# The first y load of a multiply-and-GELU kernel, issued from the ACT queue beside the first x load

## Chip, cores and metric

One core of a Trainium2 chip. The metric is device time in microseconds (us) of one execution. Runs of one kernel differ by 0.3% for the kernel before (120.61 to 121.00 us); every run used here was fast, with a granted clock of 1.0. The experiments ran on three chips, each beside the kernel before. A difference is called faster or slower from 2% on; smaller ones are given with their 95% interval. A ratio is the mean time of one kernel's fast runs over the mean of the other's in the same rounds, so it is not quite the ratio of the medians that are quoted beside it.

## The reference

```python
batch, dim = 1024, 4096            # x, y: float32
z = x * y
return 0.5 * z * (1 + np.tanh(np.sqrt(2 / np.pi) * (z + 0.044715 * z ** 3)))
```

Two inputs of 16.8 MB are read and one output of 16.8 MB is written: 50.3 MB for eight multiplies and eight activations.

## The kernel before

Each tensor is viewed as 128 partitions of 32768 numbers. x and the result live in one buffer of that size; y comes through a ring buffer of half the size. I call the two x loads x0 and x1 (8.4 MB each) and the three y loads y0 (8.4 MB), y1 and y2 (4.2 MB each). `_hoist` moves a DMA issue ahead of the start-up barriers, the points at which the engines wait for one another before the kernel's own work (in the profile before, the two hoisted issues start at 0.00 and 0.43 us and the next one, x1's, at 1.92).

The profile's names: SP is SyncE, ACT is ScalarE, DVE is VectorE, POOL is GpSimd; SPq and ACTq are their instruction queues. What SyncE issues stands in these profiles under DMA queue q1, what ScalarE issues under q10 (41.94 and 8.39 MB in the changed kernel), and the page counts 16 DMA engines for both. A packet is one record of moved bytes. I call what one DMA engine moves of one queue a ring. Each transfer has 16 records of four bytes (112 for the 7 transfers before), by their count one from each DMA engine; I call them its completion signals, and it has landed when all 16 have come. `...` marks what is left out.

```python
X_LOADS = [(0, 16384), (16384, 32768)]
Y_LOADS = [(0, 16384, 0), (16384, 24576, 0), (24576, 32768, 8192)]
STEP = 4096
STORES = [(0, 16384), (16384, 32768)]
...
    _hoist(nc, [load_x(0).ins, load_y(0).ins])       # both on SyncE's queue
    load_x(1)
    for i in (1, 2):      # y1 after 2 multiplies, y2 after 4
        nc.sync.wait_ge(sem_mul, (Y_LOADS[i][1] - Y_LOADS[1][0]) // STEP)
        load_y(i)
...
    # for each y load: wait for the x and the y load, then per 4096 columns:
    #   VectorE multiplies, ScalarE applies the GELU
...
    for i, (a, b) in enumerate(STORES):              # after 4 and after 8 activations
        nc.sync.wait_ge(sem_act, b // STEP)
        nc.sync.dma_start(out=out_r[:, a:b], in_=xs[:, a:b]).then_inc(sem_o[i], 16)
```

Of the kernel before, what the change touches and what calls it, by code (L numbers as in the profile page):

```python
# [1 line left out]

# [4 lines left out]


F32 = mybir.dt.float32
GELU = mybir.ActivationFunctionType.Gelu_apprx_tanh  # L10
# [7 lines that stand above are left out]
Y_RING = 16384  # L18


def _hoist(nc, issued):

    here = nc.cur_bb.bb.instructions
    first = nc.main_func.blocks[0].instructions
    for ins in issued:
        del here[next(k for k, i in enumerate(here) if i is ins or i.name == ins.name)]
    engine = issued[0].engine
    at = next(
        k
        for k, i in enumerate(first)  # L30
        if i.engine == engine and type(i).__name__ == "InstDrain"
    )
    first[at:at] = issued


@with_exitstack
def kernel(
    ctx: ExitStack,
    tc: tile.TileContext,
    x: bass.AP,  # L40
    y: bass.AP,
    out: bass.AP,
):
    nc = tc.nc
    P = nc.NUM_PARTITIONS

    x_r = x.flatten_outer_dims().rearrange("(p a) c -> p (a c)", p=P)
    y_r = y.flatten_outer_dims().rearrange("(p a) c -> p (a c)", p=P)
    out_r = out.flatten_outer_dims().rearrange("(p a) c -> p (a c)", p=P)
    total_f = x_r.shape[1]  # L50


    tc.close()
    tc.compile()  # L54

    xs = nc.alloc_sbuf_tensor("xs", [P, total_f], F32).ap()
    ys = nc.alloc_sbuf_tensor("ys", [P, Y_RING], F32).ap()
    sem_x = [nc.alloc_semaphore(f"sem_x{i}") for i in range(len(X_LOADS))]
    sem_y = [nc.alloc_semaphore(f"sem_y{i}") for i in range(len(Y_LOADS))]
    sem_mul = nc.alloc_semaphore("sem_mul")  # L60
    sem_act = nc.alloc_semaphore("sem_act")
    sem_o = [nc.alloc_semaphore(f"sem_o{i}") for i in range(len(STORES))]

    def load_x(i):
        a, b = X_LOADS[i]
        return nc.sync.dma_start(out=xs[:, a:b], in_=x_r[:, a:b]).then_inc(sem_x[i], 16)  # L66

    def load_y(i):
        a, b, r = Y_LOADS[i]
        return nc.sync.dma_start(  # L70
            out=ys[:, r : r + b - a], in_=y_r[:, a:b]
        ).then_inc(sem_y[i], 16)

    _hoist(nc, [load_x(0).ins, load_y(0).ins])
    load_x(1)
    for i in (1, 2):
        nc.sync.wait_ge(sem_mul, (Y_LOADS[i][1] - Y_LOADS[1][0]) // STEP)
        load_y(i)

    n = 0  # L80
    for i, (a, b, r) in enumerate(Y_LOADS):
        for j, (xa, xb) in enumerate(X_LOADS):
            if xa <= a < xb:
                nc.vector.wait_ge(sem_x[j], 16)
        nc.vector.wait_ge(sem_y[i], 16)  # L85
        for c in range(a, b, STEP):
            nc.vector.tensor_mul(  # L87
                out=xs[:, c : c + STEP],
                in0=xs[:, c : c + STEP],
                in1=ys[:, r + c - a : r + c - a + STEP],  # L90
            ).then_inc(sem_mul, 1)
            n += 1
            nc.scalar.wait_ge(sem_mul, n)
            nc.scalar.activation(  # L94
                out=xs[:, c : c + STEP], in_=xs[:, c : c + STEP], func=GELU
            ).then_inc(sem_act, 1)

    for i, (a, b) in enumerate(STORES):
        nc.sync.wait_ge(sem_act, b // STEP)
        nc.sync.dma_start(out=out_r[:, a:b], in_=xs[:, a:b]).then_inc(sem_o[i], 16)  # L100
    for i in range(len(STORES) - 1):
        nc.sync.wait_ge(sem_o[i], 16)
    nums = sorted(s.num for s in [*sem_x, *sem_y, *sem_o[:-1], sem_mul, sem_act])
    assert nums == list(range(nums[0], nums[-1] + 1))
    nc.sync.sem_clear(range(nums[0], nums[-1] + 1))
    nc.sync.wait_ge(sem_o[-1], 16).then_inc(sem_o[-1], -16)


# [1 line left out]
_INS = ['x', 'y']  # L110
_OUTS = [((1024, 4096), 'float32')]


# [23 lines left out]
```

## Time and profile before

| | before |
|---|---|
| time, median of the first 3 runs | 120.87 us (120.85 to 120.92) |
| span in the profile | 119.3 us |
| VectorE / ScalarE busy | 29% / 25% |
| share of the 16 DMA engines' time with a packet | 98.7% |
| first multiply starts | 41.31 us |
| x1 landed; y1, y2 landed | 60.5; 70.3, 80.6 us |
| the two stores landed | 100.0, 119.3 us |

A landing is the issue's start plus the time to landing in that tensor's view. The rows that matter for the bound are the DMA digits (mean busy share of the 16 engines in forty slices, in tenths) and the queue row. The lines are in the prediction. One line each of the views of the x input and of the y buffer before:

```profile
DMA to landing us min/median/max: 21.9/40.3/58.6
```

```profile
DMA to landing us min/median/max: 20.2/21.9/40.8
```

In the first line the smallest is x0, the largest x1; in the second they are y1, y2 and y0, in this order. x0 is complete at 21.9 us, and nothing uses it until y0 is there too.

### The profile page before, as it was taken

The page shows a single profiled execution, that of the slowest core. Times are in us where ns is not written, and L with a number is a line of the kernel's source. Part 1 is how long each engine was busy: PE and PEld are TensorE (multiplying, and loading weights), DVE is VectorE, ACT ScalarE, POOL GpSimd, SP SyncE. Part 2 cuts the span into 40 slices and gives each one's busy share as a digit, 9 for nine tenths or more (in the row PEclk, how much of TensorE's full clock was granted, in tenths as well). Part 3 has the DMA queues.
Part 4 walks back from the last instruction along what each step waited for, and adds up shares of the span by engine and source line. Part 5 has one row for each costly group of instructions (what it writes and reads, how often), then busy time and mean ns, then how long its engine had stood idle before and what let it go on. Part 6 is the DMA issues. An engine that isn't in the chain of part 4 may idle for free.

```text
span 119.3 us, 68 instructions
## 1 busy us (share of the span) xinstructions
DVE 35.0 (29%) x8; ACT 30.2 (25%) x9; POOL 0.2 (0%) x4
## 2 busy tenths in 40 slices
DVE  0000000000000199999600049959990000000000
ACT  3000000000000006797790000977479200000000
POOL 0000000000000000000000000000000000000000
DMA  9899888998899889988898989998889888998894
GB/s 352 352 439 615 352 352 352 659 396 352 352 615 439 352 352 483 571 352 352 385 494 352 505 374 494 385 527 352 352 352 703 352 352 352 637 418 352 352 527 176
DMA packets 1008, 50.33 MB, mean 422 GB/s; under 512 B 112, under 2 KB 112, under 8 KB 112
## 3 DMA queue, kind: packets, MB, share of 16 engines
q1 hardware_dynamic: 1008, 50.33, 98.7%
HBM read 33.55 MB, written 16.78 MB: 422 GB/s over the span
## 4 chain that ended last, share of the span: by engine, by line
DMA 53%; DVE 22%; ACT 3%; SPq 0%; issue 0%; DVEq 0%
DMA ys<-in_y_dram 53%; DVE xs L87 22%; ACT xs L94 3%; SPq L66 0%; DVEq L85 0%
## 5 line engine op out<-in xcount | busy, mean ns | idle before, releaser
L87 DVE TENSOR_TENSOR xs<-xs,ys 128x4096 f32<-128x4096 f32 x8 | 35.0, 4420 | 54.5 <-DMA ys<-in_y_dram 54.5
L94 ACT ACTIVATE xs<-xs 128x4096 f32<-128x4096 f32 x8 | 28.9, 3617 | 61.0 <-DVE xs L87 61.0
L94 ACT ACT_TABLE_LOAD x1 | 1.3, 1283 | 1.9 <-PEq L54 1.9
L121 POOL MEMSET const-uint8-127<- 128x1 uint8 x1 | 0.1, 102 | 0.0
L121 POOL MEMSET const-bfloat16-1.0<- 128x1 bf16 x1 | 0.1, 101 | 0.0
L121 POOL MEMSET const-float32-0.0<- 128x1 f32 x1 | 0.1, 98 | 0.2 <-issue 0.2
L121 POOL MEMSET const-float32-1.0<- 128x1 f32 x1 | 0.1, 98 | 0.0
## 6 DMA issues: line engine op xcount, KB each, us to landing
ys<-in_y_dram SPq DMA_DIRECT2D x2, 4096.0 KB, 21.0
xs<-in_x_dram SPq DMA_DIRECT2D x2, 40.3
out_dram<-xs SPq DMA_DIRECT2D x2, 31.8
ys<-in_y_dram SPq DMA_DIRECT2D x1, 40.8
```

Source lines behind the costliest of these rows:

```text
L87: nc.vector.tensor_mul(out=xs[:, c : c + STEP], in0=xs[:, c : c + STEP], in1=ys[:, r + c - a : r + c - a + STEP],).then_inc(sem_mul, 1)
L94: nc.scalar.activation(out=xs[:, c : c + STEP], in_=xs[:, c : c + STEP], func=GELU).then_inc(sem_act, 1)
L121: nc = _bacc.Bacc("TRN2", target_bir_lowering=False, num_devices=1)
```

## The change

The intent: do not queue y0's issue behind x0's on SyncE, but start both at once from two engines, since the first multiply needs both.

```diff
-    def load_y(i):
+    def load_y(i, engine=nc.sync):
         a, b, r = Y_LOADS[i]
-        return nc.sync.dma_start(
+        return engine.dma_start(
             out=ys[:, r : r + b - a], in_=y_r[:, a:b]
         ).then_inc(sem_y[i], 16)
 
-    _hoist(nc, [load_x(0).ins, load_y(0).ins])
+    _hoist(nc, [load_x(0).ins])
+    _hoist(nc, [load_y(0, nc.scalar).ins])
```

## The prediction

> **What bounds the kernel now.** I read the page first, for the busy shares; then the chain of work that ended last, for the path; then the issues-to-landing rows and each tensor's own view, for when each transfer arrived.
>
> ```profile
> DVE 35.0 (29%) x8; ACT 30.2 (25%) x9; POOL 0.2 (0%) x4
> ...
> DMA  9899888998899889988898989998889888998894
> ...
> DMA packets 1008, 50.33 MB, mean 422 GB/s; under 512 B 112, under 2 KB 112, under 8 KB 112
> ...
> q1 hardware_dynamic: 1008, 50.33, 98.7%
> ```
>
> The compute engines are busy for less than a third of the span. The row of DMA digits never drops below 8 before the last slice, and the one queue's packets cover 98.7% of the 16 engines' time. So the 16 DMA engines are the bound, and the time is bytes over rate plus a little at the two ends.
>
> ```profile
> 0.00 0.38 SPq L66
> 0.38 0.05 issue
> 0.43 40.78 DMA ys<-in_y_dram
> ...
> 41.31 17.44 DVE xs L87 x4
> 58.75 0.02 issue
> 58.77 21.87 DMA ys<-in_y_dram
> ...
> 80.73 8.77 DVE xs L87 x2
> ```
>
> This is the beginning and middle of the chain (columns: start, length, what). It names the first y load as the first long link: issued at 0.43 us, landed at 41.21. A reader could conclude that an earlier y load shortens the chain by 0.4 us. It does not follow: for the whole of those 40.78 us the engines move bytes, first those of x0 (first x load), then those of y0 (first y load). The chain follows the signal that came last; what set the pace is the full DMA row above it.
>
> ```profile
> 1.92 0.33 SPq L66 DMA_DIRECT2D xs<-in_x_dram  x1
> ...
> 50.10 9.00 SPq L70 DMA_DIRECT2D ys<-in_y_dram  x2
> ...
> 62.41 31.10 SPq L100 DMA_DIRECT2D out_dram<-xs  x2
> ```
>
> These timeline rows give the other issues: x1 at 1.92, y1 at 50.10 and y2 at 58.77, the stores at 62.41 and 93.17. With the times to landing (x 21.9 and 58.6; y 40.8, 20.2 and 21.9; stores 37.6 and 26.1) the landings are x0 21.9, y0 41.2, x1 60.5, y1 70.3, y2 80.6, store 0 100.0 and store 1 119.3. The six differences are 19.3, 19.3, 9.8, 10.3, 19.4 and 19.3 us: all 8 MB transfers take the same 19.3 us and the 4 MB ones half of it. Loads and stores line up in one file with hardly a hole.
>
> **The unit.** 1008 packets less the 112 tiny ones (the completion signals, 16 for each of 7 transfers) leave 896, so 128 for each transfer, 8 for each engine. 19.34 us over 8 is 2.42 us a packet, which is what the packet records show for 64 KB. The span is then 48 such units (x 16, y 16, stores 16), 116.1 us, plus 3.2 us: 1.0 from the first issue to the first byte, 0.7 by which the very first packets are longer (3.1 us), 0.9 at the last y load, which takes 10.3 to 10.6 and not 9.7 as the first store comes up behind it, and 0.35 at the end.
>
> [...]
>
> **The change part by part.**
> 1. Removed from SP: one issue of 0.43 us ahead of its start-up drain. SP should come to the barriers that much earlier, so x1 and the activation-table load may be issued at about 1.5 us and not 1.92. Neither sits on the path: x1 has x0 ahead of it on the ring, and the table (1.28 us) is needed at 45.8.
> 2. Added to ACT: one issue of about 0.4 us ahead of its own drain, which stood at 0.13 us. ACT has nothing to do until the first multiply is done, so this costs 0 on the path. The instruction order confirms that the copy is ACT's first instruction and that nothing else moves.
> 3. y0 is ready about 0.3 us earlier than 0.43. The engines get their first byte of x0 at 1.0 us either way and are then full for 40 us, so this gains at most part of the 0.7 us by which the first packets are long, if the second ring fills the hole. I count 0 to 0.4.
> 4. The order of bytes. Before: eight x0 packets, then eight y0 packets, then x1. After: x0 and y0 alternate, since they are on different rings. x0 then lands near 40 and not 21.9; y0 near 41 as before. The multiply needs both, so it still starts after 16 units: 1.0 + 0.7 + 16 x 2.42 = 40.4, plus the signal, near 41.2. **Earlier issue buys no earlier start.**
> 5. x1 is next on SP's ring behind x0. If SP is one packet ahead when x0 ends, one x1 packet per engine may slip in before the last y0 packet. The first multiply is then at 41.3 + 2.4 = 43.7. What that costs at the end is read from slack: y1 is issued after two multiplies at 50.1, but its bytes begin only when x1 has landed, at about 60; taking 1.0 us of lead off, the first multiply may slip 8.9 us before an engine starves. y2 has about 10 us, store 0 about 17. Store 1 hangs on y2's landing, not on the first multiply, and has 99.6 - 1.0 - 93.2 = 5.4 us. So even a slip of 2.4 us costs nothing.
> Sum: 0 to -0.4 us at the start and 0 later; the unit count stays 48. I choose 120.8.
>
> **The rivals.**
> - *The second ring disturbs the stream.* If each change of ring cost what the first packet lost, 0.7 us, sixteen changes would give 11 us and 132 us in all. For it: no trace here has two rings. Against it: the stretch is large packets of 64 KB, over which a change is small beside 2.42 us, and the transfers behind one another on one ring show no gap at all. A few hundredths of a microsecond per change would give +0.5 us, which the range holds.
> - *No turns: SP's ring is favoured.* x0 and x1 would move first and y0 land near 60.5. The multiplies would start there, y1 be issued at 69.3 and its bytes begin at 70.3 with the engines idle from 60: about +10 us, 131 us. [...] The mirror image, y0 first, leaves all as it was.
> - *The load is hidden anyway, and the start gets shorter.* If the two rings overlapped the start of the first packets, at most 0.7 us would come back: 120.2. The claim of a gain over 2% would need 2.4 us, and all that lies outside the 48 units is 3.2 us, of which the change touches 1.7 at most. That rules it out almost wholly.
> - *Launch overhead outside the span* is now 1.3 to 1.6 us (120.63 to 120.87 against 119.3); a second queue in use may add some tenths.
>
> **Range and chances.** The middle is the time before less a trace of the start. The low end takes most of the 0.7 us; the high end takes 0.04 us per change of ring or a few tenths of overhead. The two bad rivals together get 4%, a gain over 2% gets 1%.
>
> **What would show it.** Two queues in the queue rows, the new one with 8.4 MB; x0's time to landing near 40 us and not 21.9 (turns, step 4); first multiply between 41.0 and 43.7 (steps 4, 5); the DMA row still at 8 and 9 all along, or above where records of two rings overlap; y1, y2 and both stores landing within 0.5 us of 70.3, 80.6, 100.0 and 119.3; x1 issued near 1.5 (step 1). I am wrong if the packets get longer while two rings are active, or if the DMA row shows a hole near 60 us.

The sum, whose parts are read from the profile before, came to 0 to -0.4 us at the start and 0 later, from 120.87 us, and I chose 120.8. Without a ground is the alternation in step 4, and with it the weight against "no turns": at that time an assumption of mine, first shown by the changed kernel's packet records below. The 0.04 us for a change of ring and the tenths for a second queue were guesses, put to the test below.

## The result, and the profile after

The changed kernel takes 120.80 us (median of 6 runs, 120.56 to 121.04) against 120.86 (6 runs, 120.66 to 120.92): ratio 0.9997, 95% interval 0.9982 to 1.0013. No gain or loss shows; the interval leaves 0.2% either way. The page of the changed kernel:

```profile
DVE 35.0 (29%) x8; ACT 30.2 (25%) x9; POOL 0.2 (0%) x4
...
DMA  9899889988899889988999989998899888998893
...
q1 hardware_dynamic: 864, 41.94, 82.4%
q10 hardware_dynamic: 144, 8.39, 16.2%
```

There are now two queues, the second with exactly y0's 8.39 MB. The two shares add to 98.6%, before 98.7%: the engines are as full as they were. The chain of waits after (start, length, what):

```profile
0.12 41.33 DMA ys<-in_y_dram
...
41.55 17.44 DVE xs L88 x4
59.00 0.02 issue
59.01 21.90 DMA ys<-in_y_dram
...
81.01 8.77 DVE xs L88 x2
```

y0 is issued 0.31 us earlier (0.12, before 0.43) and takes 0.55 us longer (41.33, before 40.78). Its landing is thus 0.24 us later in this one profile. Three runs that share the start of the kernel before differ by 0.16 us in the first multiply (41.31 to 41.47), so one profile does not settle whether the 0.24 is real. By the packet records the last bytes of y0 moved at 40.90 us, before 40.85; the rest of the 0.24 lies between these and the signal's arrival. The issues, from the timeline after:

```profile
0.00 1.90 SPq L66 DMA_DIRECT2D xs<-in_x_dram  x2
0.12 0.36 ACTq L70 DMA_DIRECT2D ys<-in_y_dram  x1
...
50.34 9.00 SPq L70 DMA_DIRECT2D ys<-in_y_dram  x2
...
62.66 31.12 SPq L101 DMA_DIRECT2D out_dram<-xs  x2
```

The group of two x issues ends at 1.90 with the second, so x1's issue starts near 1.56 and not 1.92: SyncE and with it the barriers are early by about the issue that it lost (0.43 us before; ScalarE's table load behind the barriers starts at 1.57 us, before 1.92). The later issues are all where they were, to 0.3 us, and so are the landings: y1 70.3, y2 80.9, the stores 100.2 and 119.6 us. The view of the x input after shows where the earlier start of y0 went:

```profile
DMA to landing us min/median/max: 41.3/50.2/59.1
```

x0 now lands at 41.3 and not at 21.9. By the packet records below, y0 got every second packet and x0 lost those turns. Both loads end together (41.3 and 41.5 us) where formerly the second one ended (41.2).

The packet records say it packet by packet: in the first 40 us all packets of the sixteen engines come in sixteen rounds of 16, x0 (q1), y0 (q10), x0, y0 and so on, of 2.42 us each (the very first round 3.06 us in the mean; before, 3.12; in seven other runs that start with packets of this size, 3.10 to 3.26).

### The profile page after: what moved, and what is told of

Same layout as the page of the kernel before. It is cut to its first block, busy times and chain, and to the rows that moved or that the text cites. A ratio compares the mean times of both kernels' runs of the same rounds, so it can differ in the third digit from the quotient of the medians.

```text
span 119.6 us, 68 instructions
## 1 busy us (share of the span) xinstructions
DVE 35.0 (29%) x8; ACT 30.2 (25%) x9; POOL 0.2 (0%) x4
## 3 DMA queue, kind: packets, MB, share of 16 engines
q10 hardware_dynamic: 144, 8.39, 16.2%
## 4 chain that ended last, share of the span: by engine, by line
DMA 53%; DVE 22%; ACT 3%; issue 0%; DVEq 0%
DMA ys<-in_y_dram 53%; DVE xs L88 22%; ACT xs L95 3%; DVEq L86 0%
## 6 DMA issues: line engine op xcount, KB each, us to landing
ys<-in_y_dram ACTq DMA_DIRECT2D x1, 41.3
```

## The experiments

My theory going in: the engines move one file of packets without a hole, so the time is the number of packets; order matters only where it lets an engine starve, and between the first multiply and the end there are 8.9 us of slack. The rivals: the moment of an issue counts by itself; the chain of waits is the path, so any delay of the first multiply counts in full; changes of ring cost time that the slack hides.

### y0 from ACT, but after the barriers

```diff
-    _hoist(nc, [load_y(0, nc.scalar).ins])
+    load_y(0, nc.scalar)
```

> One part of the change undone: y0 is still issued from ACT, but after the start-up barriers (about 1.5 us) and no longer at the same moment as x0. My theory (the engines are full from 1.0 us on, the two rings take turns, only byte order changes): time 120.8 within 0.4 us, first multiply within 0.5 us of the 41.55 of the changed kernel, x0 landing near 41 again. Rival (the moment of the issue is what counts, a later one costs its delay): y0 and with it the end about 1.4 us later, 122.2 us.

Measured: 120.82 us, ratio to before 0.9998 (0.9983 to 1.0014). The timeline of this run:

```profile
1.44 0.37 ACTq L70 DMA_DIRECT2D ys<-in_y_dram  x1
...
43.85 17.43 DVE L88 TENSOR_TENSOR xs<-xs,ys 128x4096 f32<-128x4096 f32 x4 [43.85 <-DMA ys<-in_y_dram]
```

The time is as my theory had it, so "at the same moment" is worth nothing. But the first multiply came 2.3 us later than in the changed kernel, where I had allowed 0.5. The rival's 1.3 us of later issue is not the number either; 2.3 us is nearly one packet. The packet records show why. Here the earliest record of each round near the end of y0 (start in us, ring, bytes; q1 is SyncE's, q10 ACT's):

```
35.43  q10  65536   y0
37.84  q1       4   x0's completion signal
37.85  q10  65536   y0, its last bytes
40.27  q1   65536   x1
42.68  q10      4   y0's completion signal
```

SyncE's ring was two packets ahead, for the first two rounds were both x0's, so x0 ended a round early. Why y0 missed the second round (it started at 4.02 to 4.75 us, and y0's issue had ended at 1.81) is not settled. In the run with small packets on two rings, below, ACT's first packet came at 2.95 us, 2.83 us after its issue began; an estimate from this puts y0's first packet here at 4.3 us, too late for the engines that began the second round first. All of y0's bytes had moved by 40.97 us on the slowest engine. Its signal, four bytes, came after the next packet of x1. **The completion signal looked like a packet of its own that waits for its ring's turn:** in the records above y0's bytes ended at 40.27 us and its signal came at 42.68, one x1 packet later. That was a new theory, tested at the end. In the changed kernel the same records read x0, y0, x0's signal, y0's signal, x1: no x1 packet between, which is why x0 landed at 41.3 (its bytes had moved by 38.49 us, and its signal, which waited one round for y0's last packet, is recorded from 40.15 on) and y0 was not delayed.

### 2 MB and 6 MB of x1 ahead of y0

Both are the kernel before with the same bytes in another order on SyncE's ring; the first multiply is made late by a set amount.

```diff
-X_LOADS = [(0, 16384), (16384, 32768)]
+X_LOADS = [(0, 16384), (16384, 20480), (20480, 32768)]   # or cut at 28672
...
-    _hoist(nc, [load_x(0).ins, load_y(0).ins])
-    load_x(1)
+    _hoist(nc, [load_x(0).ins, load_x(1).ins, load_y(0).ins])
+    load_x(2)
...
-            if xa <= a < xb:
+            if xa < b and xb > a:
```

> The kernel before with 2 MB of x1 moved ahead of y0 on SP's ring, the same bytes in all: y0 lands 4.8 us later. My theory (8.9 us of slack between the first multiply and the end): first multiply near 46.1, end unchanged, 120.9 us within 0.5. Rival A (the reported chain of waits is the path, each us of the first y load counts in full): 125.7 us.

> The same with 6 MB of x1 ahead of y0: y0 lands 14.5 us later, past the slack. My theory: first multiply near 55.8, y1 issued at 64.6 while the last of x1 has landed at 60.5, a hole of 5.6 us in the DMA row near 60 to 66 us, time 126.5 us within 0.8. Rival A (chain is the path): 135.4 us. Rival B (only the number of bytes counts, the order never): 120.9 us.

Measured: 120.93 us with 2 MB, ratio 1.0008 (0.9988 to 1.0028); 128.57 us with 6 MB, ratio 1.062 (1.0576 to 1.0665). With 2 MB, from the timeline:

```profile
46.33 17.43 DVE L87 TENSOR_TENSOR xs<-xs,ys 128x4096 f32<-128x4096 f32 x4 [46.33 <-DMA ys<-in_y_dram]
```

The first multiply is 5.0 us late and the kernel is not, so the chain of waits is not the path. With 6 MB, the page's DMA row and then a stretch of the table by windows (after the stretch and its length: VectorE, ScalarE and GpSimd busy time, clock, DMA share, GB/s):

```profile
DMA  9797796996999799777058998998988998998990
```

```profile
60.20:65.60 5.40, 5.40 (x3) 4.51 (x2) 0.00 (x0) 1.00 0.00 0
```

The row has the hole that the slack predicts: for 5.4 us nothing moves, because y1 may only be issued after two multiplies, at 64.7. So the slack is real and bounded, and "only bytes count" fails as surely as "only the chain counts". My 126.5 was 2 us short, though. The landings say where: y1 lands 6.4 us later than before (76.7 against 70.3), so 1.0 more than the hole; y1's first packets after it take 1.3 to 2.1 us (1.8 in the mean) and not 1.21, which is 0.6 of it. y2 lands another 1.5 us later (88.5, before 80.6), as its own packets are stretched more than before. So this run lost more than the idle time; that the part in y2 follows from the hole is not shown (the stretching of y2 is taken up below).

### x1, not y0, issued beside x0

The same change made to the wrong load.

```diff
-    load_x(1)
+    _hoist(nc, [load_x(1, nc.scalar).ins])
```

`load_x` is given an engine as a second argument, as `load_y` is in the changed kernel.

> The kernel before with x1, not y0, issued from ACT at the same moment as x0; x0 and y0 stay on SP. If the engines take the two rings in turn: x0 and x1 share the first 40 us, y0 comes alone after them and lands near 60.5, first multiply 60.6, y1 issued near 69.4, a hole of about 10 us in the DMA row, time near 131.1 us within 1. If an engine empties the ring that was filled first (SP) before the other: x0 and y0 land by 41.2 and the time stays 120.9 us.

Measured: 132.98 us, ratio 1.1001 (1.0975 to 1.1028). The page's DMA row, one row of the timeline, and the stretch without traffic in the table by windows:

```profile
DMA  9897997987977979970007899899879879799791
```

```profile
60.70 17.43 DVE L87 TENSOR_TENSOR xs<-xs,ys 128x4096 f32<-128x4096 f32 x4 [60.70 <-DMA ys<-in_y_dram]
```

```profile
60.10:70.40 10.30, 9.70 (x3) 4.52 (x2) 0.00 (x0) 1.00 0.00 0
```

The rings took turns here too: x0 and x1 landed at 41.3 and 41.4 us, y0 after them at 60.6. Nothing moves for the 10.3 us from 60.1 to 70.4, and as above some 2 us come on top (0.8 in y1, whose first packets after the hole take 1.4 to 1.95 us, and 1.2 in y2, by their landings). So two rings do change what happens, and can cost a tenth of the time: the load put beside x0 took turns from it (x0 landed at 41.3 us, before 21.9), and so delayed what stood behind it, here y0 (60.6, before 41.2).

### Small packets, on one ring and on two

x0 and y0 are each cut into eight loads of 1 MB with rows of 8 KB. First all on SyncE, then x0 on SyncE and y0 on ACT.

```diff
-    _hoist(nc, [load_x(0).ins, load_y(0).ins])
+    _hoist(nc, pieces(xs, x_r, nc.sync, sem_x[0]) + pieces(ys, y_r, nc.sync, sem_y[0]))
```

`pieces` issues the eight loads, 2048 columns each, on the engine that it is given. The second has `nc.scalar` for y0's pieces, hoisted on ACT; the waits on these two semaphores are for 128 in place of 16 in both.

> The kernel before with x0 and y0 each cut into eight loads of 1 MB (8 KB rows, so 64 small packets an engine for each in place of 8 large ones), all on SP's ring. Baseline for the next run. Both theories: 120.5 to 123 us, depending on what 8 KB packets cost.

> The same small loads, x0's from SP and y0's from ACT, as in the changed kernel: some 128 changes of ring in place of 16 if a turn is one packet. My theory (a change of ring costs nothing measurable): within 0.5 us of the run with small loads on one ring, first multiply within 0.5 us too. Rival (a change costs some 0.04 us and is only hidden in the width of the range): about 5 us longer over the first 41 us, still hidden at the end by the slack of 8.9 us but plain in the first multiply.

Measured: 120.89 us on one ring, ratio to before 0.9999 (0.9983 to 1.0016), and 120.94 on two, 1.0013 (0.9988 to 1.0039). Timelines, one ring and then two:

```profile
42.21 17.43 DVE L97 TENSOR_TENSOR xs<-xs,ys 128x4096 f32<-128x4096 f32 x4 [42.21 <-DMA ys<-in_y_dram]
```

```profile
49.52 17.43 DVE L98 TENSOR_TENSOR xs<-xs,ys 128x4096 f32<-128x4096 f32 x4 [49.52 <-DMA ys<-in_y_dram]
```

The windows from 10 to 20 us, one ring and then two (the last two columns are the DMA share and GB/s):

```profile
10.00:20.00 10.00, 0.00 (x0) 1.28 (x1) 0.00 (x0) 1.00 1.01 425
```

```profile
10.00:20.00 10.00, 0.00 (x0) 0.00 (x0) 0.00 (x0) 1.00 1.01 424
```

The end is the same, but the first multiply on two rings is 7.3 us later, where I had expected 0.5 and the rival about 5. It looks like the rival's size and is not its mechanism. A packet takes 0.31 us in both runs from 2.5 us on, and the rates agree, so changing rings cost nothing measurable (424 GB/s against 425). What delays y0 comes after 41 us: SyncE's ring had a lead of about three packets an engine from the first 5 us (43 + 69 packets against 58, over 16 engines), so x0 was done first, and from then on each small packet of y0 had to wait for one 64 KB packet of x1. y0 had two packets and a signal left: three turns of 2.42 us are 7.3; the records have y0's last packets from 43.17 and 45.89 us on and its signals from 48.62 on. **In these records a turn was one packet, of 8 KB (0.31 us) as of 64 KB (2.42 us).** It stayed free only because of the slack; y1 was issued at 58.3, and x1 landed at 61.5.

### The store held until y2 has landed

My sum had 0.9 us for "the last y load, as the first store comes up behind it". This asks whether the store does it.

```diff
     for i, (a, b) in enumerate(STORES):
+        nc.sync.wait_ge(sem_y[2], 16)
```

> The kernel before with the first store held until y2 has landed, to ask what makes y2 take 10.4 us and not 9.7. If it is the store queued behind it: y2 lands 9.7 us after y1, near 80.0 us, the engines then wait some 1.0 us for the store, time about 121.8 us. If it is y2 itself (say, the multiplies beside it): y2 lands near 80.6 as before and the time is about 122.8 us.

Measured: 121.48 us, ratio 1.0049 (1.0034 to 1.0064). The view of the y buffer:

```profile
DMA to landing us min/median/max: 20.2/21.2/40.8
```

The median is y2's: 21.2 us, before 21.9. With no store queued behind it, y2's packets all take 1.21 us, where before its last two on each engine took 1.8 to 2.2 and 1.2 to 1.4. y2 lands at 80.0 as expected, and the gap before the store (no bytes from 79.56 to 80.85 us, 1.3 us where I had expected 1.0) costs more than was won: 120.89 less 0.7 plus 1.3 is the 121.5 measured. The 121.8 that I had expected was 0.3 too high and does not follow from its own parts. The stretch came with the store queued early (y2 landed 10.4 us after y1) and not in this run without it (9.7). An early store is not enough alone: in all three runs with small packets, the two above and the last one below, the store was queued too (at 63.3, 70.6 and 62.9 us), and y2 landed 9.7 us after y1. In the other runs with an early store it landed 10.2 to 10.6 us after y1, and 11.6 to 11.8 in the two runs with a hole, where the store was issued 1.2 us after y2's bytes had begun to move. Why it was spared here and stretched more there stays open. After the gap of 1.3 us the store's first packets took 2.44 to 2.46 us against 2.42, so the longer first packets after the holes of 5.4 and 10.3 us (1.3 to 2.1 against 1.21) did not come after every gap.

### The first store held until five activations are done

If queueing the store early does harm and late leaves a gap, the best moment is in between: about 1 us, an issue's lead (in the profile before, x0's first packet started 1.0 us after its issue), before y2's bytes end.

```diff
-        nc.sync.wait_ge(sem_act, b // STEP)
+        nc.sync.wait_ge(sem_act, max(b // STEP, 5))
```

> The kernel before with the first store held until five activations are done (issue near 78.5 us in place of 62.4), so that it joins the ring just before y2's last bytes have moved. It is asked whether the 0.7 us that y2 loses with the store queued behind it can be had back without the gap that the run with the store held for y2's landing left. If the store must be queued early to stretch y2: y2 lands near 80.0, time 120.2 us. If any store that follows without a gap stretches it: y2 near 80.6, time 120.9 us within 0.2.

Measured: 120.07 us (5 runs, 119.78 to 120.19) against 120.82, ratio 0.9928 (0.9914 to 0.9941). From the timeline and the view of the y buffer:

```profile
78.63 14.45 SPq L100 DMA_DIRECT2D out_dram<-xs  x2
```

```profile
DMA to landing us min/median/max: 20.2/21.3/40.9
```

The store is issued at 78.63 and not 62.41, y2's time to landing is 21.3 us as without a store behind it, and the store's packets start at 79.48 to 79.84 us, as y2's end (79.19 to 79.84). This is the only version here that is faster than the kernel before by more than the noise: 0.7%, under the 2% line. It was not run with the change of this document in it. Issuing a transfer *later* gained what issuing one earlier did not.

### y0 after the barriers, x1 in small loads

The test of the waiting signal: as in the first experiment, but the packet that the signal would wait for is 8 KB.

```diff
-    load_x(1)
+    for c in range(16384, 32768, 2048):   # eight loads; the wait is for 128
+        nc.sync.dma_start(out=xs[:, c : c + 2048], in_=x_r[:, c : c + 2048]).then_inc(
+            sem_x[1], 16
+        )
```

> The run with y0 issued after the barriers, but x1 behind x0 cut into eight loads of 1 MB (8 KB rows). In that run all of y0's bytes had moved by 41.0 us and only its completion signal came at 43.1 to 43.8, behind one 64 KB packet of x1. If a completion signal waits for a turn of its ring like any packet: here it waits for one 8 KB packet, 0.3 us, and the first multiply starts near 41.8 us. If the 2.3 us are the price of the later issue of y0: it starts near 43.9 us as in that run. Time 120.9 us within 0.5 either way, for the slack holds it.

Measured: 120.70 us, ratio 0.9990 (0.9977 to 1.0004). From the timeline:

```profile
1.44 0.37 ACTq L70 DMA_DIRECT2D ys<-in_y_dram  x1
...
41.74 17.43 DVE L91 TENSOR_TENSOR xs<-xs,ys 128x4096 f32<-128x4096 f32 x4 [41.74 <-DMA ys<-in_y_dram]
```

The first multiply is back at 41.74, with y0 still issued at 1.44. The records have y0's signals from 40.74 us on, after one 8 KB packet of x1 that started at 40.44. The 2.3 us were the signal's wait for a 64 KB packet, not the price of the later issue.

## Why the prediction was right

- **The bound.** The full DMA row was read as the limit, and the chain's first link as the last signal only. Shown: the first multiply was moved by +0.2, +2.5, +5.0 and +8.2 us against before (41.55, 43.85, 46.33 and 49.52, against 41.31), and the time stayed the same (ratios 0.9997 to 1.0013). One reading was too wide: the engines moved bytes for 40.2 of the 40.78 us, the first packet having started at 1.00.
- **The unit.** The 48 units of 2.42 us held. The sum for the rest did not add up: its four terms make 2.95 us and not 3.2, and 0.25 us stays unexplained. The 0.9 for y2 is 0.7 by the landings (10.4 us after y1, less 9.7).
- **Steps 1 to 3, the issues.** x1's issue came at 1.56, predicted near 1.5; y0's was 0.31 us earlier, predicted about 0.3. Neither shortened the time. Of the 0 to 0.4 us allowed for filling the slow first packets next to nothing came: their mean went from 3.12 to 3.06 us, less than three runs with the start of the kernel before differ by (3.10 to 3.21).
- **Step 4, turns.** Strict alternation (sixteen rounds of 2.42 us), which the prediction had assumed and no run had shown by then. The first multiply at 41.55 lies in the stated 41.0 to 43.7. x0's landing was a little mis-sized: "near 40", measured 41.3, since I put x0's landing at its last bytes and not at its signal, which waits a round.
- **Step 5, the slip.** "One x1 packet per engine may slip in before the last y0 packet" did not happen in the changed kernel. When it did, with the later issue, it went before y0's signal and not before its bytes; the 2.4 us were right, the object was not.
- **Slack.** 8.9 us was the estimate. A slip of 8.2 us cost nothing, one of 14.6 us left a hole of 5.4, so the slack was about 9.2 us. What the estimate lacked is that the two runs with a hole lost some 2 us beyond its length.
- **What the number alone does not show.** With this slack the time comes out the same when the first multiply slips by up to 8.2 us, as other runs show, and by the prediction's own account it would have if all of y0 had moved first. A time of 120.8 alone is thus weak support. The mechanism rests on x0's landing, the packet records and the runs with x1 beside x0 and with 6 MB ahead, not on the time.
- **The rivals.** "The second ring disturbs the stream" falls: the same packet time, 0.31 us, with about 128 changes of ring as with none. "No turns" falls with x1 beside x0 (ratio 1.1001). "The start gets shorter" falls with the start as it was. No added overhead outside the span shows: 120.91 less 119.6 is 1.3 us in the profiled run, as before (120.63 less 119.3).

## What to carry to other kernels

In these runs a second issuing engine gave no second set of DMA engines: they were full before and after (98.7% and 98.6%), and the two loads that are needed together ended no earlier than the second had ended before. So look at the DMA row before counting on an earlier issue. Check instead what each transfer stands in front of: putting the wrong load beside the first made the time 10% longer, while letting a store into the queue just in time rather than early gained 0.7%. Where two rings shared the engines here, a load in 8 KB packets beside one in 64 KB packets was held up 7.3 us, so compare the packets of the load that is waited for with those it competes with. Its completion signal waited for a turn too: the first multiply came 2.3 us later behind a 64 KB packet, 0.2 us behind one of 8 KB.
